# Weights of layer 1 and of both output projections split once ahead of use, kept in DRAM in two parts, and loaded in both parts

## The chip, the core and the metric

One NeuronCore of a Trainium2 chip runs the whole program in one launch. The metric is the device time in microseconds (us) of one execution, median of three. The engines are TensorE (PE, matrix products; PEld is its weight load), VectorE (DVE), ScalarE (ACT), GpSimd (POOL) and SyncE (SP), which here issues nearly all DMA transfers. Each engine works through its own instruction list in order and waits on semaphores.

## What is computed

Two layers of a streaming encoder in fp32, for 2048 prompt frames and 64 frames of a running stream (width D = 1024, 8 heads). Cut to what matters here:

```python
def hgrn_layer(x, S0, ...):                      # layer 0
    q, fx, i, z = jnp.split(rms_norm(x) @ w_in, 4)   # w0: 1024 x 4096
    f = lb + (1 - lb) * sigmoid(fx); k = 1 - f
    o, S = gla(q, k, i, log(f), S0)              # gated linear attention, blocks of 16
    return x + (rms_norm(o) * silu(z)) @ w_out   # wo0: 1024 x 1024

def diff_attn_layer(x, k_past, v_past, ...):     # layer 1
    q, k, v, z = jnp.split(rms_norm(x) @ w_in, 4)    # w1: 1024 x 4096
    p = softmax(rms_norm(q) @ rms_norm(k).T * 64 ** -0.5 - slope * dist)  # two maps per head
    o = (p[:, 0] - lam * p[:, 1]) @ v
    return x + (rms_norm(o) * (1 - lam_init) * silu(z)) @ w_out  # wo1: 1024 x 1024
```

Prompt frames attend causally by chunks of 64; the 64 sample frames attend to 2048 cached keys. Outputs are both layers' result, the new keys and values and the new states.

## The kernel before, in words

**Precision.** Each fp32 product is made of fp32r products: an operand is held as a high part (rounded to fp32r) and a low part (the rest), and `mm3` (L110 to L112) adds hi·hi, hi·lo and lo·hi. So every weight tile has to be split once: `split_w` copies the raw tile to the high half of a tile `w` of 128x2048 (ACT, L132) and subtracts that from the raw tile into the low half (L135, on POOL, on DVE, or half on each). For the output projections ACT first multiplies the raw tile by a scale per row (L131).

**Layer 0** (before about 1050 us) runs four chunks of 512 frames; in each, eight steps, one for each head: projection, gated scores, values, norm. In chunk 0 the w0 weights are loaded raw (`want`, `load_raw`), split, used, and stored in both parts in the DRAM tensor `w0_d`. Chunks 1 to 3 load both parts from there as 1 MB (`w<-w_d`) into a ring of NRING = 6 tiles. A step lasts some 24 us; the first and fifth step of a chunk, which also project values for four heads, last some 46 us. Then comes the output projection of layer 0 (`out_units`), whose eight weight tiles are loaded raw (0.5 MB) and split near the last steps of chunk 3.

**Layer 1** runs head after head, 17 tiles of frames each (16 of 128 prompt frames and one of the 64 sample frames), some 181 us a head: `project`, `turn`, `scores`, `values` and `norms` of different tiles, mixed by a plan that is written out for PE. Each tile's input `ht` is loaded from `h1_d`. The four weight tiles of the next head are loaded raw and split while the last tiles of a head are projected (`raw1` at tile NT-4, `split1` at tiles NT-2 and NT-1, subtractions half on DVE, half on POOL). The six first tiles of the second output projection are split the same way at the end of the last head (`split1` with h = H, on POOL), and the last two when attention ends (`open_rest`). Attention of the sample frames over the cache and the output projection follow.

**Order.** PE's order is written by hand (`manual_schedule`). The order on DVE, ACT, POOL and SP is chosen by the scheduler from the dependences, within the bounds that the pools set: a tile with `bufs=3` takes one of three buffers in turn, and its writer waits until the buffer's last reader is done. `dma` (L54) puts every transfer on SP's one list.

## Time and profile before

| | before |
|---|---|
| median of 3 executions | 3035.18 us (3032.98 to 3035.47) |
| the profiled execution | 3037.97 us, of which the span from first to last instruction is 3035.9 us |
| mean granted TensorE clock | 0.983 |
| busy share of the span | PE 96%, PEld 80%, DVE 65%, ACT 44%, POOL 25% |
| DMA | 494.10 MB, mean 163 GB/s |

The profile was taken on one execution, 2.8 us above the median; sums are made against 3037.97 us and then moved by that difference. Busy shares are means over stages that differ much: layer 0 to about 1056 us, its output projection to about 1263 us, layer 1's heads to about 2720 us, then the sample frames and the output projection.

### The profile page before, as it was taken

The page shows a single profiled execution, that of the slowest core. Times are in us where ns is not written, and L with a number is a line of the kernel's source. Part 1 is how long each engine was busy: PE and PEld are TensorE (multiplying, and loading weights), DVE is VectorE, ACT ScalarE, POOL GpSimd, SP SyncE. Part 2 cuts the span into 40 slices and gives each one's busy share as a digit, 9 for nine tenths or more (in the row PEclk, how much of TensorE's full clock was granted, in tenths as well). Part 3 has the DMA queues.
Part 4 walks back from the last instruction along what each step waited for, and adds up shares of the span by engine and source line. Part 5 has one row for each costly group of instructions (what it writes and reads, how often), then busy time and mean ns, then how long its engine had stood idle before and what let it go on. Part 6 is the DMA issues. An engine that isn't in the chain of part 4 may idle for free.

```text
span 3035.9 us, 49261 instructions
## 1 busy us (share of the span) xinstructions
PE 2917.5 (96%) x17258; PEld 2423.9 (80%) x17258; DVE 1974.7 (65%) x5598; ACT 1339.1 (44%) x3089; POOL 754.1 (25%) x841
## 2 busy tenths in 40 slices
PE   7999999999999899999999999999999999979898
PEld 5778888887899788787888878788887888867666
DVE  4765546546454744478687786868778686772673
ACT  3332122212211322356565565656656565553562
POOL 4330000000000200233333333332332333333451
PEclk8999999999999999999999999999999999989899
DMA  9554444444334266754444445444453544525653
GB/s 351 191 215 165 168 157 143 181 156 146 129 115 151 102 224 218 245 177 138 159 140 156 158 136 164 142 155 136 144 178 121 162 135 155 160 84 162 201 168 120
DMA packets 196679, 494.10 MB, mean 163 GB/s; under 512 B 27088, under 2 KB 114000, under 8 KB 161360
## 3 DMA queue, kind: packets, MB, share of 16 engines
q1 hardware_dynamic: 196432, 490.95, 48.3%
q8 instruction: 137, 2.24, 0.3%
q14 instruction: 110, 0.90, 0.1%
HBM read 352.45 MB, written 104.86 MB: 151 GB/s over the span
## 4 chain that ended last, share of the span: by engine, by line
PE 85%; DVE 7%; issue 2%; DMA 2%; POOL 2%; ACT 1%; SPq 0%; DVEq 0%; ACTq 0%; POOLq 0%
PE psproj L110 19%; PE psproj L112 18%; PE psproj L111 18%; PE psX L807 4%; PE psX L808 4%; PE psX L852 3%; PE psS L404 2%; PE psO L111 2%; PE psO L110 2%; PE psO L112 2%; PE psX L103 1%; DVE e L811 1%; PE psX L519 1%; PE psX L768 1%; DMA gs<-g_d 1%
## 5 line engine op out<-in xcount | busy, mean ns | idle before, releaser
L110 PE MATMUL psproj<-w,ht 128*128 128x512 f32 x1024 | 429.9, 420 | 0.3 <-DVE e L831 0.3
L112 PE MATMUL psproj<-w,ht 128*128 128x512 f32 x1024 | 403.7, 394 | 0.0
L111 PE MATMUL psproj<-w,ht 128*128 128x512 f32 x1024 | 403.7, 394 | 0.0
L816 ACT ACTIVATE e<-e,st 128x1024 f32<-128x1024 f32 (+7 forms) x384 | 343.2, 898 | 107.4 <-DVE st L811 107.3
L110 PE MATMUL psproj<-hT,w 128*128 128x512 f32 (+1 forms) x960 | 361.4, 376 | 0.0
L111 PE MATMUL psproj<-hT,w 128*128 128x512 f32 (+1 forms) x960 | 340.0, 354 | 0.0
L112 PE MATMUL psproj<-hT,w 128*128 128x512 f32 (+1 forms) x960 | 339.7, 354 | 0.0
L89 POOL TENSOR_TENSOR rs<-var,mhalf 128x4 f32<-128x4 f32 (+3 forms) x208 | 203.1, 978 | 432.0 <-DVE var L88 227.8
L811 DVE CUSTOM_DVE_ANT_0 e<-psX,dist,st 128x512 f32<-128x512 f32 (+3 forms) x384 | 248.1, 646 | 65.7 <-PE psX L808 59.8
L807 PE MATMUL psX<-kg,qt 128*128 128x512 f32 (+3 forms) x640 | 244.2, 382 | 6.8 <-DVE at L855 6.1
L854 ACT ACTIVATE at<-psX 128x512 fp32r<-128x512 f32 (+2 forms) x320 | 169.6, 531 | 168.2 <-PE psX L852 166.6
L808 PE MATMUL psX<-kg,qt 128*128 128x512 f32 (+3 forms) x640 | 237.5, 371 | 0.0
L811 DVE CUSTOM_DVE_ANT_0 e<-psX,dist 128x512 f32<-128x512 f32 (+3 forms) x256 | 163.0, 637 | 106.1 <-PE psX L808 104.0
L855 DVE TENSOR_TENSOR at<-psX,at 128x512 fp32r<-128x512 f32 (+2 forms) x320 | 193.7, 606 | 53.5 <-ACT at L854 51.6
L112 PEld LDWEIGHTS psproj<-w,ht 128*128 128x128 f32 x1024 | 192.5, 188 | 44.9
L110 PE MATMUL psproj<-w,gs 128*128 128x512 f32 x512 | 214.4, 419 | 7.0 <-ACT gs L573 7.0
L112 PE MATMUL psproj<-w,gs 128*128 128x512 f32 x512 | 206.2, 403 | 7.3 <-DVE gs L575 6.2
L111 PEld LDWEIGHTS psproj<-w,ht 128*128 128x128 f32 x1024 | 194.2, 190 | 15.8
L110 PEld LDWEIGHTS psproj<-w,ht 128*128 128x128 f32 x1024 | 193.7, 189 | 16.2 <-DVE st L829 0.7
L135 POOL TENSOR_TENSOR w<-wraw,w 128x1024 fp32r<-128x1024 f32 (+1 forms) x80 | 163.2, 2047 | 167.9 <-ACT w L132 158.1
L110 PEld LDWEIGHTS psproj<-hT,w 128*128 128x128 f32 x960 | 181.5, 189 | 29.1
L111 PE MATMUL psproj<-w,gs 128*128 128x512 f32 x512 | 204.4, 399 | 0.0
(245 smaller groups left out, 6618.6 us busy)
## 6 DMA issues: line engine op xcount, KB each, us to landing
ht<-h_d SPq DMA_DIRECT2D x128, 1024.0 KB, 5.1
w<-w_d SPq DMA_DIRECT2D x96, 1024.0 KB, 4.9
w_d<-w SPq DMA_DIRECT2D x32, 1024.0 KB, 4.9
qt<-qx SPq DMA_DIRECT2D x512, 64.0 KB, 2.1
gs<-g_d SPq DMA_DIRECT2D x44, 512.0 KB, 4.1
wraw<-in_w SPq DMA_DIRECT2D x32, 512.0 KB, 4.5
h_d<-hs SPq DMA_DIRECT2D x16, 1024.0 KB, 4.1
out_kvp<-raw SPq DMA_DIRECT2D x128, 128.0 KB, 1.8
```

The source lines that it names most:

```text
L89: G.tensor_tensor(out, v[:np_, :n], mhalf[:np_, :n], ALU.pow)
L110: T.matmul(out, l[0], r[0], start=first, stop=False)
L111: T.matmul(out, l[0], r[1], start=False, stop=False)
L112: T.matmul(out, l[1], r[0], start=False, stop=last)
L135: e.tensor_tensor(w[:, x * m:(x + 1) * m, 1], raw[:, x * m:(x + 1) * m], w[:, x * m:(x + 1) * m, 0], ALU.subtract)
L807: T.matmul(s[:, :w], qt[:, m, 0], kgt[:, m, :w], start=True, stop=False)
L808: T.matmul(s[:, :w], qt[:, m, 1], kgt[:, m, :w], start=False, stop=True)
L811: V.tensor_tensor_reduce(out=e[:, o:o + w], in0=s[:, :w], in1=dist[:, x0:x0 + w], scale=slope, scalar=3e38 if b["prev"] is None else b["pr ...
L816: A.activation(b["e"][m, hf][:, :n], b["e"][m, hf][:, :n], AF.Exp, bias=mn, scale=-1.0, accum_out=st4[:, 8 + 2 * hf + m:9 + 2 * hf + m])
L852: T.transpose(t[:, k * P:(k + 1) * P], b["a"][r][kt // 8][:, (kt % 8) * P:(kt % 8 + 1) * P], ident)
L854: A.activation(at[:, 0, :n, r], tv, AF.Copy)
L855: V.tensor_tensor(at[:, 1, :n, r], tv, at[:, 0, :n, r], ALU.subtract)
```

## The change

The weights of layer 1 and of both output projections (48 raw tiles of 0.5 MB) get the treatment of layer 0's own: 48 units `presplit`, two to a step, are written into the steps of chunks 1 to 3. Each loads a raw tile, makes the high part on ACT (two 128x512 copies) and the low part on DVE in place (two 128x512 subtractions), and stores both to new DRAM tensors `wo_d` and `w1_d` (two stores of 0.5 MB). Where these weights are used, `load_w` loads both parts as 1 MB. Raw and high parts share one tag of three buffers, which moves from the pool `wp` to `l0`. In layer 1 the next head's weights are loaded from tile NT-8 on, and the last of the four of each head after head 0 gets a buffer of its own (`wx`). `split_w` stays for w0 in chunk 0.

```diff
@@ -67,6 +67,8 @@
     h1_d = dram.tile([NT, P, 2, NK, P], F32, name="h1_d")
     sm_d = dram.tile([H, TS, 512], F32, name="sm_d")
     w0_d = dram.tile([H, 7, P, 2048], F32, name="w0_d")
+    w1_d = dram.tile([H, 4, P, 2048], F32, name="w1_d")
+    wo_d = dram.tile([2, 8, P, 2048], F32, name="wo_d")
 
     ident = const.tile([P, P], F32, name="ident")
     ones = const.tile([P, 1], F32, name="ones")
@@ -117,18 +119,22 @@
         T.matmul(out, l, r[1], start=False, stop=last)
 
     def load_raw(src, n):
-        raw = wp.tile([P, 1024], F32, tag="raw", bufs=NRAW, name="wraw")
+        raw = l0.tile([P, 1024], F32, tag="raw", bufs=NRAW, name="wraw")
         raw = raw.rearrange("p (k n) -> p k n", n=n)
         dma(raw, src)
         return raw
 
-    def split_w(raw, n, pool=None, scale=None, engines=(G,)):
-
-        w = (pool or wp).tile([P, 2048], F32R, tag="w", bufs=2 if pool else NRING, name="w")
+    def load_w(src, n, pool=None, tag="w", bufs=None):
+
+        w = (pool or wp).tile([P, 2048], F32R, tag=tag, bufs=bufs or NRING, name="w")
+        dma(w.bitcast(F32), src)
+        return w.rearrange("p (k a n) -> p k a n", a=2, n=n)
+
+    def split_w(raw, n, engines=(G,)):
+
+        w = wp.tile([P, 2048], F32R, tag="w", bufs=NRING, name="w")
         w = w.rearrange("p (k a n) -> p k a n", a=2, n=n)
         nk = 1024 // n
-        for k in range(nk if scale is not None else 0):
-            A.activation(raw[:, k], raw[:, k], AF.Copy, scale=scale[:, k:k + 1])
         A.activation(w[:, :, 0], raw, AF.Copy)
         m = nk // len(engines)
         for x, e in enumerate(engines):
@@ -192,13 +198,10 @@
             c, h, s = key = wlist[wnext[0]]
             wnext[0] += 1
             if c != "out" and c > 0:
-                w = wp.tile([P, 2048], F32R, tag="w", bufs=NRING, name="w")
-                dma(w.bitcast(F32), w0_d[h, s])
-                n = P if s < 3 else 512
-                ws[key] = w.rearrange("p (k a n) -> p k a n", a=2, n=n)
+                ws[key] = load_w(w0_d[h, s], P if s < 3 else 512)
                 continue
             if c == "out":
-                ws[key] = split_w(load_raw(out_src(0, h, s), 512), 512, scale=osc[:, 0, 2 * s:2 * s + 2])
+                ws[key] = load_w(wo_d[0, 4 * h + s], 512)
             elif s < 3:
                 ws[key] = split_w(load_raw(I["w0h"][h, s].rearrange("p (k n) -> p k n", k=NK), P), P, engines=engines)
             else:
@@ -206,6 +209,36 @@
                 ws[key] = split_w(load_raw(I["w0v"][h // 4, k:k + 2].rearrange("k p n -> p k n"), 512), 512, engines=engines)
             if c == 0:
                 dma(w0_d[h, s], ws[key].rearrange("p k a n -> p (k a n)").bitcast(F32))
+
+
+    plist = [(0, n) for n in range(8)] + [(2 + h, k) for h in range(H) for k in range(4)] + [(1, n) for n in range(8)]
+
+    def presplit(x):
+
+        ly, n = plist[x]
+        b = {}
+
+        def load():
+            src = out_src(ly, n // 4, n % 4) if ly < 2 else I["w1"][ly - 2, 2 * n:2 * n + 2].rearrange("k p n -> p k n")
+            b["raw"] = load_raw(src, 512)
+
+        def split():
+            raw = b["raw"]
+            hi = l0.tile([P, 1024], F32, tag="raw", bufs=NRAW, name="whi").rearrange("p (k n) -> p k n", n=512)
+            dst = (wo_d[ly, n] if ly < 2 else w1_d[ly - 2, n]).rearrange("p (k a n) -> p k a n", a=2, n=512)
+            for k in range(2):
+                h, r = hi[:, k].bitcast(F32R), raw[:, k]
+                if ly < 2:
+                    sc = osc[:, ly, 2 * (n % 4) + k:2 * (n % 4) + k + 1]
+                    A.activation(h, r, AF.Copy, scale=sc)
+                    V.scalar_tensor_tensor(out=r.bitcast(F32R), in0=r, scalar=sc, in1=h, op0=ALU.mult, op1=ALU.subtract)
+                else:
+                    A.activation(h, r, AF.Copy)
+                    V.tensor_tensor(r.bitcast(F32R), r, h, ALU.subtract)
+            dma(dst[:, :, 0], hi)
+            dma(dst[:, :, 1], raw)
+
+        return [(1, load), (1, split)]
 
     def norm0(c, n):
         ti = cxs[c]["tiles"][n]
@@ -633,21 +666,17 @@
             units += [(0.43, lambda g=g: turn(ti, g)) for g in range(2)]
         return units
 
-    def raw1(h, k):
-
-        if h < H:
-            ctxs[h]["raw"][k] = load_raw(I["w1"][h, 2 * k:2 * k + 2].rearrange("k p n -> p k n"), 512)
-        elif k < NRING:
-            cx1["raw"][k] = load_raw(out_src(1, k // 4, k % 4), 512)
-
-    def split1(h, k):
-        if h < H:
-            ctxs[h]["w"][k] = split_w(ctxs[h]["raw"].pop(k), 512, engines=(V, G))
-        elif k < NRING:
-            cx1["w"][k // 4, k % 4] = split_w(cx1["raw"].pop(k), 512, scale=osc[:, 1, 2 * (k % 4):2 * (k % 4) + 2])
-
-    cx1 = dict(ly=1, w={}, raw={})
-    ctxs = {h: dict(w=[None] * 4, kg={}, v={}, q={}, z={}, ht={}, raw={}) for h in range(H)}
+    def load1(h, k):
+
+        if h == H:
+            cx1["w"][k // 4, k % 4] = load_w(wo_d[1, k], 512)
+        elif h > 0 and k == 3:
+            ctxs[h]["w"][k] = load_w(w1_d[h, k], 512, r1, "wx", 1)
+        else:
+            ctxs[h]["w"][k] = load_w(w1_d[h, k], 512)
+
+    cx1 = dict(ly=1, w={})
+    ctxs = {h: dict(w=[None] * 4, kg={}, v={}, q={}, z={}, ht={}) for h in range(H)}
 
     s1, s1b, r0s, r1s, so = (ExitStack() for _ in range(5))
     r1 = l1 = l1e = l1b = psum1 = None
@@ -702,15 +731,16 @@
             else:
                 mm2(cx["pp"], cx["ht"][i][:, 0, k], rhs, k == 0, k == NK - 1)
             if k % 2:
-                if i == NT - 4 and k < 4:
-                    raw1(h + 1, k // 2)
-                if i == NT - 2 and k < 4:
-                    split1(h + 1, k // 2)
-                    raw1(h + 1, k // 2 + 2)
-                if i == NT - 1 and (k < 4 or h == H - 1):
-                    split1(h + 1, k // 2 + 2)
-                    if h == H - 1:
-                        raw1(H, k // 2 + 4)
+
+                early = [0, 1] + [2] * (h > 0) + [3] * (h == 0)
+                if NT - 8 <= i < NT - 8 + len(early) and k == 3:
+                    load1(h + 1, early[i - NT + 8])
+                if i == NT - 1 and h == H - 1 and k < 6:
+                    load1(H, 3 + k // 2)
+                elif i == NT - 1 and h == 0 and k == 1:
+                    load1(1, 2)
+                elif i == NT - 1 and 0 < h < H - 1 and k == NK - 1:
+                    load1(h + 1, 3)
             if k == NK - 1:
                 cx["ht"].pop(i)
                 finish(cx["pp"])
@@ -1068,7 +1098,7 @@
         s1.close()
         op2, cx1["split"] = pool(s3, "op2"), V
         for k in range(NRING, 8):
-            cx1["w"][1, k % 4] = split_w(load_raw(out_src(1, 1, k % 4), 512), 512, pool=op2, scale=osc[:, 1, 2 * (k % 4):2 * (k % 4) + 2])
+            cx1["w"][1, k % 4] = load_w(wo_d[1, k], 512, op2, bufs=2)
         open_decode()
 
     def open_rows():
@@ -1115,7 +1145,8 @@
                 for _, step in main[:2] + side[:1]:
                     step()
                 main, side = main[2:], side[1:]
-            weave((0, 1, main), (0, 1, side))
+            x = 2 * (n - H)
+            weave((0, 1, main), (0, 1, side), (0, 1, presplit(x) + presplit(x + 1) if c else []))
             if h == 1 and c > 0:
                 rms0(c - 1)
         sh.close()
@@ -1124,7 +1155,7 @@
         work0 = [(ti, (0, 1)) for ti in [0, 1, 2, NT - 1] + list(range(3, NT - 1))]
         out_load(cx0, *work0[0])
         for n in range(NRING, 8):
-            cx0["w"][1, n % 4] = split_w(load_raw(out_src(0, 1, n % 4), 512), 512, pool=op, scale=osc[:, 0, 2 * (n % 4):2 * (n % 4) + 2])
+            cx0["w"][1, n % 4] = load_w(wo_d[0, n], 512, op, bufs=2)
         cx0["wbc"] = op.tile([P, D], F32, tag="wbc", bufs=1, name="wbc1")
         dma(cx0["wbc"], I["norm_bc"][1])
         weave((0, 0.9, side0(*steps[-1])), (OPS, 1, out_units(cx0, work0, 0, ps0) + out_units(cx0, work0, 1, ps0)))
@@ -1143,15 +1174,11 @@
         op_last = ub[16:]
         out_load(cx0, *work0[-1])
         load_ht(0)
-        for k in range(2):
-            raw1(0, k)
         for _, step in ua[:6] + prev[:1] + ua[6:8] + ub[:1] + prev[1:] + ub[1:8]:
             step()
+        for k in range(4):
+            load1(0, k)
         dma(dist, I["dist"])
-        for k in range(4):
-            split1(0, k)
-            if k < 2:
-                raw1(0, k + 2)
         for _, step in ua[8:16] + ub[8:13] + last[:1] + ub[13:15] + last[1:] + ub[15:16]:
             step()
         for _, _, step in sorted(plan, key=lambda x: x[:2]):
```

In the built programs PE has the same instructions in the same order. On DVE the 96 subtractions stand from the fifth head of chunk 0 to the fourth head of chunk 2, since the scheduler moves them ahead of their place in the text; the order shows no presplit in chunk 3. Names carry buffer numbers, which differ between the two; line numbers too (L396 of the change is L363 of before, L446 is L413, L841 is L811, L861 is L831, L885 is L855, L801 is L771).

DVE in chunk 1, where the products of keys k with decays F of one step are made, before:

```order
L363 TENSOR_TENSOR k_3026<-k_3026,F_3250 128x128x2
L413 COPY_PREDICATED attc_3251<-masks_92,psS_3296 128x64x2
L363 TENSOR_TENSOR k_3026<-k_3026,F_3250 128x64x4
L413 COPY_PREDICATED attc_3251<-masks_92,psS_3296 128x32x4 x2
L363 TENSOR_TENSOR k_3026<-k_3026,F_3250 128x32x8
L413 COPY_PREDICATED attc_3251<-masks_92,psS_3354 128x16x8
L363 TENSOR_TENSOR k_3026<-k_3026,F_3250 128x16x16
L413 COPY_PREDICATED attc_3251<-masks_92,psS_3354 128x8x16 x2
L363 TENSOR_TENSOR Q_3252<-Q_3252,F_3250 128x8x32
L363 TENSOR_TENSOR k_3026<-k_3026,F_3250 128x8x32
L363 TENSOR_TENSOR Q_3252<-Q_3252,F_3250 128x4x64
L363 TENSOR_TENSOR k_3026<-k_3026,F_3250 128x4x64
```

and the same place with the change (L237 is the presplit's subtraction):

```order
L237 TENSOR_TENSOR wraw_5173<-wraw_5173,whi_5220 128x512 x2
L237 TENSOR_TENSOR wraw_5295<-wraw_5295,whi_5359 128x512 x2
L396 TENSOR_TENSOR k_3082<-k_3082,F_3324 128x32x8
L446 COPY_PREDICATED attc_3325<-masks_94,psS_3430 128x16x8
L396 TENSOR_TENSOR k_3082<-k_3082,F_3324 128x16x16
L446 COPY_PREDICATED attc_3325<-masks_94,psS_3430 128x8x16 x2
L237 TENSOR_TENSOR wraw_5403<-wraw_5403,whi_5450 128x512 x2
L396 TENSOR_TENSOR Q_3326<-Q_3326,F_3324 128x8x32
L396 TENSOR_TENSOR k_3082<-k_3082,F_3324 128x8x32
L396 TENSOR_TENSOR Q_3326<-Q_3326,F_3324 128x4x64
L396 TENSOR_TENSOR k_3082<-k_3082,F_3324 128x4x64
L237 TENSOR_TENSOR wraw_5535<-wraw_5535,whi_5624 128x512 x2
```

Four presplits, eight subtractions, now stand between or just around the products k<-k,F of one step; PE's score products wait for these.

SP at the start of layer 1, before (ht is a tile's input, h_d what turn stores, x_d the residual, wraw raw weights, out_kvp an output of keys and values):

```order
L54 DMA wraw_10863<-in_w1 128x2x512
L54 DMA wraw_12213<-in_w1 128x2x512
L54 DMA wraw_12235<-in_w1 128x2x512
L54 DMA wraw_12509<-in_w1 128x2x512
L54 DMA x1_d_65<-xt_10701 128x1024
L54 DMA wraw_12543<-in_w1 128x2x512
L54 DMA wraw_14425<-in_w1 128x2x512
L54 DMA x1_d_65<-xt_10776 128x1024
L54 DMA h1_d_66<-hs_10923 128x2048
L54 DMA ht_11028<-h1_d_66 128x2048
L54 DMA ht_11072<-h1_d_66 128x2048
L54 DMA h1_d_66<-hs_10981 128x2048
L54 DMA out_kvp<-raw_11000 128x256
```

and with the change:

```order
L54 DMA w_11244<-w1_d_69 128x2048
L54 DMA w_11246<-w1_d_69 128x2048
L54 DMA w_11248<-w1_d_69 128x2048
L54 DMA x1_d_65<-xt_11095 128x1024
L54 DMA w_12096<-w1_d_69 128x2048
L54 DMA w_12227<-w1_d_69 128x2048
L54 DMA x1_d_65<-xt_11170 128x1024
L54 DMA h1_d_66<-hs_11301 128x2048
L54 DMA h1_d_66<-hs_11359 128x2048
L54 DMA out_kvp<-raw_11378 128x256
L54 DMA ht_11406<-h1_d_66 128x2048
L54 DMA ht_11450<-h1_d_66 128x2048
```

The 0.5 MB raw loads are 1 MB loads of both parts, and the two ht loads that stood ahead of the last h1_d store now come behind it and behind the first out_kvp store, which waits for POOL.

DVE at one of the seven changes of head, near 1590 us in the trace of before (e, st and at belong to the softmax of the last tiles of one head), before:

```order
L135 TENSOR_TENSOR w_14896<-wraw_14721,w_14896 128x512
L831 SCALAR_TENSOR_TENSOR e_14706<-e_14774,st4_14705,e_14706 128x1024
L831 SCALAR_TENSOR_TENSOR e_14736<-e_14831,st4_14705,e_14736 128x640
L811 ISA e_14917,st4_14881<-psX_14935,dist_9715,st4_14881 128x256
L811 ISA st4_14881 128x1
L135 TENSOR_TENSOR w_14924<-wraw_14755,w_14924 128x512
L855 TENSOR_TENSOR at_14928<-psX_14929,at_14928 128x3x128
L771 SCALAR_TENSOR_TENSOR qx_14947<-psX_14944,wq_98,qx_14947 128x128
L811 ISA e_14962,st4_14881<-psX_14963,dist_9715 128x512
L811 ISA st4_14881 128x1
L135 TENSOR_TENSOR w_16929<-wraw_16637,w_16929 128x512
L811 ISA e_14962,st4_14881<-psX_14972,dist_9715,st4_14881 128x512
```

and with the change:

```order
L861 SCALAR_TENSOR_TENSOR e_15070<-e_15126,st4_15069,e_15070 128x1024
L861 SCALAR_TENSOR_TENSOR e_15094<-e_15183,st4_15069,e_15094 128x640
L841 ISA e_15265,st4_15233<-psX_15279,dist_10109,st4_15233 128x256
L841 ISA st4_15233 128x1
L885 TENSOR_TENSOR at_15272<-psX_15273,at_15272 128x3x128
L801 SCALAR_TENSOR_TENSOR qx_15291<-psX_15288,wq_100,qx_15291 128x128
L841 ISA e_15306,st4_15233<-psX_15307,dist_10109 128x512
L841 ISA st4_15233 128x1
L841 ISA e_15306,st4_15233<-psX_15316,dist_10109,st4_15233 128x512
L841 ISA st4_15233 128x1
L841 ISA e_15329,st4_15233<-psX_15330,dist_10109,st4_15233 128x512
L841 ISA st4_15233 128x1
```

The subtractions of L135 are gone, and the softmax rows stand in the same order.

## Rows read from the trace of the kernel before

**Rows 1.** PE's waits, whole span: for what, us in total, times, longest.

```profile
PE psX L852 <- DVE st L811: 13.7, 8, 3.0
...
PE psX L852 <- DVE e L831: 11.0, 8, 4.4
...
PE psX L807 <- DVE at L855: 6.1, 7, 1.8
```

**Rows 2.** Layer 0: us, busy PE PEld DVE ACT POOL, clock, DMA share, GB/s.

```profile
0.00:50.00 50.00, 34.62 (x135) 26.87 (x136) 18.22 (x43) 21.45 (x32) 18.89 (x16) 0.86 0.92 342
...
450.00:700.00 250.00, 250.00 (x1675) 201.01 (x1674) 135.18 (x400) 56.38 (x119) 13.20 (x13) 1.00 0.44 159
```

**Rows 3.** Groups by line: busy us, mean ns of one, idle before and releaser.

```profile
L135 POOL TENSOR_TENSOR w<-wraw,w 128x1024 fp32r<-128x1024 f32 (+1 forms) x80 | 163.2, 2047 | 167.9 <-ACT w L132 158.1 <-PE psX L489 6.7 <-PE psproj L112 2.7
...
L131 ACT ACTIVATE wraw<-wraw,osc 128x512 f32<-128x512 f32 x32 | 21.5, 714 | 8.8 <-DMA wraw<-in_wo 8.7
```

**Rows 4.** End of layer 0, DVE, POOL in order of time: start us, us, operation.

```profile
1017.09 0.52 DVE L363 TENSOR_TENSOR k<-k,F 128x256 f32<-128x256 f32 x2
...
1042.16 3.77 DVE L363 TENSOR_TENSOR k<-k,f 128x256 f32<-128x256 f32 x2
...
1046.63 4.09 DVE L363 TENSOR_TENSOR k<-k,F 128x256 f32<-128x256 f32 x2
...
1043.34 7.34 POOL L135 TENSOR_TENSOR w<-wraw,w 128x1024 fp32r<-128x1024 f32 x3
```

**Rows 5.** PE's waits from 1020 to 1060 us.

```profile
PE psS L404 <- DVE k L363: 7.9, 3, 5.0
```

**Rows 6.** Stretches at the lower clock, columns as in rows 2.

```profile
1051.50:1056.10 4.60, 4.56 (x25) 3.79 (x26) 3.53 (x15) 0.00 (x0) 0.00 (x0) 0.50 0.59 219
...
1595.40:1598.80 3.40, 3.24 (x11) 2.88 (x12) 3.33 (x10) 1.90 (x7) 0.00 (x0) 0.50 0.65 213
...
2697.90:2704.70 6.80, 6.59 (x27) 6.20 (x28) 5.03 (x15) 4.55 (x10) 2.71 (x4) 0.50 0.07 17
```

**Rows 7.** DVE late in one head of layer 1 and at the change to the next.

```profile
1563.68 2.08 DVE L831 SCALAR_TENSOR_TENSOR e<-e,st 128x1024 f32<-128x1024 f32 x2
...
1590.16 3.11 DVE L831 SCALAR_TENSOR_TENSOR e<-e,st 128x1024 f32<-128x1024 f32 x2
...
1596.20 0.68 DVE L135 TENSOR_TENSOR w<-wraw,w 128x512 fp32r<-128x512 f32 x1
```

**Rows 8.** PE's waits from 2680 to 2725 us, at the end of the last head.

```profile
PE psX L852 <- DVE e L831: 4.4, 1, 4.4
...
PE psX L852 <- DVE st L811: 3.0, 1, 3.0
```

**Rows 9.** Start of layer 1, SP and PE in order of time.

```profile
1268.60 4.89 SPq L54 DMA_DIRECT2D ht<-h_d  x2
...
1274.48 0.34 SPq L54 DMA_DIRECT2D out_kvp<-raw  x1
...
1275.18 0.40 PE L110 MATMUL psproj<-w,ht 128*128 128x512 f32 x1
```

**Rows 10.** DMA issues: KB each, median us from issue to landing.

```profile
ht<-h_d SPq DMA_DIRECT2D x128, 1024.0 KB, 5.1
...
wraw<-in_w SPq DMA_DIRECT2D x32, 512.0 KB, 4.5
...
wraw<-in_w0h SPq DMA_DIRECT2D x24, 512.0 KB, 6.6
```

**Rows 11.** DVE between which, by the order, the first and last presplits come.

```profile
220.53 0.28 DVE L384 COPY M<-Q 128x256 f32<-128x256 f32 x1
...
626.41 0.43 DVE L434 TENSOR_TENSOR q<-q,f 128x256 f32<-128x256 f32 x1 [1.46 <-ACT q L291]
```

**Rows 12.** The last key product of a step in chunk 1, and its user on PE.

```profile
382.24 0.42 DVE L363 TENSOR_TENSOR k<-k,F 128x256 f32<-128x256 f32 x1
...
382.89 0.68 PE L480 MATMUL psX<-Q,k 128*64 128x64 f32 x8
```

## The prediction

> **What bounds the kernel now.** I read the page first: PE is busy nearly all of the span, so a change gains only where PE waits or runs slowly, and loses wherever it makes PE wait. Then the table of stretches: in layer 0 between 450 and 700 us PE is busy 250.00 of 250.00 us, DVE (the third busy time in such a row) 135.18, ACT 56.38, and the DMA engines are at a share of 0.44 for 159 GB/s [rows 2]. Nothing is to be gained there. Then PE's waits over the whole span: the greatest in layer 1 are for softmax work of DVE, 13.7, 11.0 and 6.1 us in 7 or 8 pieces each [rows 1], one for each change of head and one for the end of the last head. There the kernel splits weights. The timeline of these places shows how: a pair of L831 that takes 2.08 us in the middle of a head takes 3.11 us at a change [rows 7], and at the end of layer 0 pairs of L363 that take 0.52 us take 3.77 and 4.09 us while POOL runs three subtractions L135 for 7.34 us [rows 4]. DVE and POOL hold each other up. Behind such waits the granted clock falls: three stretches of 4.60, 3.40 and 6.80 us were run at 0.50, the level of 1.2 GHz, with PE busy for 4.56, 3.24 and 6.59 us [rows 6]; a stretch like the second stands at each change of head.
>
> **What the change removes.** All splits of w1, wo0 and wo1 leave these places, among them 48 of POOL's 80 subtractions L135 of 2.05 us on average [rows 3] and the four on DVE at each change of head.
>
> *End of layer 0.* PE waits 7.9 us for k L363 [rows 5]. The first slow pair begins 1.2 us before POOL's L135, so of its excess 3.77 − 0.52 = 3.25 us about 2.0 are due to L135; the second pair's excess is 4.09 − 0.52 = 3.57 [rows 4]. Together 5.6 us, less than the wait. The half-clock stretch behind it costs half of 4.56 us, 2.3 [rows 6]. Term: −8 (bounds −4, if the clock falls anyway and a third of the wait stays, and −11, wait and clock whole).
>
> By the Trainium skill, page "SBUF — State Buffer", section "Who interferes with whom", a DVE operation with two SBUF inputs and a GpSimd operation that reads SBUF exclude each other for a whole instruction. The pairs above agree: 0.52 us alone, 4.09 beside L135. By that rule the new subtractions, which have two SBUF inputs as well, would be blocked where they meet POOL's remaining splits in chunk 0, where POOL is busy 18.89 of the first 50 us [rows 2]; a dozen of the 96 stand in chunk 0, and with 2.05 us [rows 3] for two in five of them that would be some 10 us of DVE time, inside the bounds for layer 0 below.
>
> *Seven changes of head.* Without the end of the last head (3.0 and 4.4 us [rows 8]) the three waits of rows 1 come to 10.7 + 6.6 + 6.1 = 23.4 us, 3.3 a change. The four L135 on DVE, 0.68 us each when undisturbed, and the 1.03 us that the pair L831 loses [rows 7] make 3.7 us of DVE time just ahead of these waits, more than the waits. I take four fifths of 23.4, since the softmax chain itself stays: 19. Half of 3.24 us of clock [rows 6] is 1.6, times seven 11. Term: −30 (−12 to −40). The new loads are 1 MB at 5.1 us [rows 10] where raw ones were 0.5 MB; three of four are issued some tiles ahead, under the products of the tiles between; the fourth goes with the head's last product and is used three quarters of a tile later, some 8 us (181 us a head over 17 tiles). I cost them at nothing; without that cover a change loses up to 5 us.
>
> *End of the last head.* Waits of 7.4 us [rows 8] and half of 6.59 us [rows 6]: −10 (−5 to −20, if the waits for gs just behind it shrink too).
>
> **What it adds.** *Start of layer 1.* The two ht loads that were issued from 1268.60 on now stand behind the first out_kvp, which went at 1274.48; so the first goes at about 1274.9 and lands 5.1 us later, at 1280.0, while PE starts on that tile at 1275.18 [rows 9, 10]. Queued behind it on PE is everything. Term: +5 (0, if out_kvp goes earlier since POOL is freer, to +9).
>
> *Start of the sample frames.* Two 1 MB loads of wo1 stand on SP's list just ahead of inputs that PE waits for; one such load lands in 5.1 us [rows 10]. +3 (0 to +6).
>
> *Layer 0.* By the order the presplits don't spread over the last three chunks: they lie between rows that start at 220.53 and 626.41 us [rows 11], 48 in some 406 us, one in 8.5 us. Three costs meet there.
>
> First, cover. Each brings two subtractions like L135, 0.68 us [rows 7], and two copies like L131, 0.71 us [rows 3]: 65 us on DVE, 69 on ACT. There is room on average, but not in the chain: the last key product ends at 382.66 and PE takes it at 382.89 [rows 12], 0.2 us of cover, and the order puts up to four presplits between such products. If one piece in six comes late by its length less the cover, 96 / 6 × 0.5 = 8 us; with the longer steps of values, better covered, I take 10.
>
> Second, the loop. Raw and high parts share three buffers, so a presplit's high part waits for the store of the raw part before it: per presplit 0.71 + 2 × 0.68 = 2.1 us of ACT and DVE and one store. The trace has no such store; the nearest rows are 0.5 MB transfers of 4.5 us and, at chunk 0's load, 6.6 us [rows 10]. So 6.6 to 8.7 us, against 8.5 that there are: slack of 1.9 at one end, short by 0.2 × 48 = 10 us at the other. As all engines go in order, a late store stops ACT and DVE, and they PE.
>
> Third, DMA. 48 × 1.57 MB in 406 us is 186 GB/s, on top of 159 makes 345, as much as the first 50 us moved at a share of 0.92 (342 GB/s) [rows 2]. So I take the loaded end, nearest in load, and with the uneven places (four in one step) 15 us for the loop. Term for layer 0: +25 (0, all covered, to +75, stores of 8 us: 10 us of cover and 48 × 1.6 rounded down).
>
> By the Trainium skill, page "DMA: Bandwidth & Descriptors", section "Where 436 GB/s comes from", HBM transfers of a core are bound at about 358 GB/s; the first 50 us (342 at 0.92) agree in order of size. By that rule the 345 fit with 4% to spare and transfers would queue, which speaks against this change: it is the mechanism of rival C, whose price and chance are worked out from the rows alone.
>
> **Sum.** −8 − 30 − 10 + 5 + 3 + 25 = −15: from 3037.97 to 3023 in a profiled execution. That execution stands 2.8 us above the median, so 3020 for the median, 0.5% faster. A measurement of this kernel can tell about 0.2%, 6 us, from no change.
>
> **Rivals.** *A, the forecast*: 3005 to 3030, chance 0.44.
>
> *B, layer 0 hides it all.* For it: DVE is busy 54%, ACT 23% and the DMA engines 44% there [rows 2], and PE has other products to do. Against: the cover of 0.2 us [rows 12]. Without the +25 the sum is −40: 2995, and down to 2980 with the ends of the gains. Chance 0.16.
>
> *C, the other side: the presplit loop paces layer 0.* If a store takes more than 6.4 us (8.5 − 2.1) under load, each of the 48 presplits is late and holds ACT, DVE and SP. The other terms come to −40; with 10 us of cover the gain is gone when 48 × (store − 6.4) = 30, at a store of 7.0 us. At 7.5 us the loop costs 53 and the sum is +23: 3058. For it: 6.6 us at chunk 0's load [rows 10] and 345 GB/s; against: layer 0's loads are issued well ahead, and PE can go on while SP is late. Chance 0.23.
>
> *D, the changes of head keep their waits.* If the softmax chain and the tile of sample frames, not L135, set them, only 12 of the 30 come, and the sum is +3: about no change, 3038. For it: the clock falls after quite short waits; against: 3.7 us of DVE time goes from just there. Chance 0.17.
>
> A and B make it faster, D in part; C slower. Faster by over 0.2%: 0.61; within: 0.16; slower: 0.23. The range 2988 to 3050 leaves out the far ends of B and C; A's own range is 3005 to 3030.
>
> **What would show it.** In the changed kernel's profile: no split of weights after chunk 0's other than the presplits; L831 pairs at about 2.1 us at the changes of head, PE's three waits of rows 1 below half, fewer half-clock stretches; a new wait of some 5 us for ht near the start of layer 1; in layer 0 from 220 to 650 us a DMA share near 0.9, PE waits for k L363's counterpart, ACT waiting for buffers of the stores, and chunk 2's end late by some 25 us. I am wrong if layer 0 is not late at all or by over 50 us, or if waits at the changes of head stay though the splits are gone.

## The result, and the profile after

The change takes 2997.72 us (median of four, 2996.45 to 3003.42) against 3034.83 us: a ratio of 0.9882, with an interval of 0.9865 to 0.9899. The profiled execution took 2998.95 us, its span 2997.1 us, against 3037.97 and 3035.9. It is 1.2% faster, where 0.5% was forecast: the direction holds, the gain is over twice the forecast one.

PE runs the same 17258 matmuls in the same order in both kernels, so the time between the same two matmuls can be compared. The table cuts the span by the times of before; "PE idle" is the change in the time that PE stood between matmuls.

| stretch of before, us | forecast | measured | of it PE idle |
|---|---|---|---|
| 0 to 220, chunk 0 | 0 | −0.6 | −0.1 |
| 220 to 1000, layer 0 | +25 | +16.1 | +12.0 |
| 1000 to 1060, its end | −8 | −6.5 | −4.7 |
| 1060 to 1262, output projection | 0 | −0.3 | −0.3 |
| 1262 to 1300, start of layer 1 | +5 | +5.3 | +3.2 |
| seven changes of head | −30 | −42.3 | −24.9 |
| 2665 to 2735, end of the last head | −10 | −12.8 | −10.4 |
| 2735 to 2830, start of the sample frames | +3 | +4.2 | +2.6 |
| 2830 to the end | 0 | −2.1 | −1.2 |

The sum is −39.0; forecast was −15. Two terms make most of the difference: the changes of head gained 12 us more, layer 0 lost 9 us less.

The table compares one execution of each kernel. The runs below repeat parts of it, and say how far each row can be trusted. The changes of head took 42.2 to 42.3 us less in all five later kernels that leave them as the change has them. Layer 0 (220 to 1000 us) took 15.2 to 20.0 us more in the six that leave it so, and repeated itself within 0.01 us in the two that are the kernel before there. Behind 2665 us single executions differ more: those same two kernels, in which nothing behind 2665 us was edited, took 16.1 and 5.8 us less for the last three rows than the profile of before, so the gain at the end of the last head is anything from 7 to 13 us.

PE's waits in the change, whole span (for what, us in total, times, longest), which answer to [rows 1]:

```profile
PE psX L513 <- DVE k L396: 7.3, 6, 2.6
...
PE psproj L112 <- DMA ht<-h_d: 4.3, 1, 4.3
...
PE psO L113 <- DVE at L885: 3.3, 8, 0.7
...
PE psX L882 <- DVE e L861: 3.1, 1, 3.1
```

The 13.7 and 6.1 us of [rows 1] are gone, the 11.0 us are down to one wait of 3.1 at the end of the last head. New are 7.3 us for key products in layer 0, one wait of 4.3 us for ht, and smaller ones. The table of stretches (length, busy PE PEld DVE ACT POOL, granted clock, DMA share, GB/s) shows layer 0 twice, the start of layer 1, one change of head and the end of the last head:

```profile
250.00:300.00 50.00, 48.00 (x324) 38.05 (x321) 33.19 (x82) 19.68 (x39) 2.07 (x2) 0.97 0.91 311
550.00:600.00 50.00, 49.59 (x305) 40.23 (x303) 31.73 (x84) 14.03 (x29) 1.50 (x1) 1.00 0.96 361
1271.20:1280.00 8.80, 8.80 (x46) 7.26 (x45) 4.48 (x8) 3.63 (x8) 0.54 (x1) 1.00 1.02 422
1579.20:1624.10 44.90, 44.08 (x259) 37.72 (x258) 39.34 (x118) 29.39 (x69) 15.50 (x19) 1.00 0.61 210
2637.10:2694.30 57.20, 49.58 (x265) 41.25 (x264) 41.97 (x111) 31.37 (x66) 17.25 (x16) 0.94 0.39 125
```

In layer 0 the DMA engines are at 0.91 and 0.96, where before they were at 0.44 [rows 2]. At the change of head PE is busy for 44.08 of 44.90 us at full clock, where a stretch at 0.50 stood [rows 6]. The pair of L831 that took 3.11 us there [rows 7] is the pair L861 now, on DVE in order of time:

```profile
1598.16 2.08 DVE L861 SCALAR_TENSOR_TENSOR e<-e,st 128x1024 f32<-128x1024 f32 x2
```

It takes what it takes in the middle of a head. Where layer 0 loses time, DVE, ACT and PE in order of time show one of the places:

```profile
387.52 0.69 DVE L237 TENSOR_TENSOR wraw<-wraw,whi 128x512 fp32r<-128x512 f32 x1 [1.68 <-ACT whi L236]
...
388.33 0.69 DVE L237 TENSOR_TENSOR wraw<-wraw,whi 128x512 fp32r<-128x512 f32 x1
```

```profile
386.86 1.16 ACT L236 ACTIVATE whi<-wraw 128x512 fp32r<-128x512 f32 x2 [2.36 <-DMA w_d<-whi]
```

```profile
391.14 0.68 PE L513 MATMUL psX<-Q,k 128*64 128x64 f32 x8 [2.60 <-DVE k L396]
```

ACT has the raw tile but waits 2.36 us for a buffer, until the store of an earlier high part is done (`w_d<-whi`); DVE waits 1.68 us for ACT, works 2 × 0.69 us on the presplit, and PE's score products wait 2.60 us for the key product behind that. The summary of ACT's line L236 (what it waited for, and who waited for it, us and times) and the transfers (KB, us to landing) say how common this is:

```profile
L236 ACT ACTIVATE whi<-wraw x64: 612/621/635, 292.3 to 568.5; 128x512 fp32r<-128x512 f32 x64
...
  DMA wraw<-in_w: 45.4, 19
  DMA w_d<-whi: 26.6, 7
...
  DVE wraw L237: 52.6, 26
```

The larger wait is for raw loads. They are late in part because SP holds them back: a load, too, needs a buffer, and SP waits for the store of the low part that is still in it. SP's own wait for these stores, 219.7 to 686.4 us:

```profile
SPq L54 <- DMA w_d<-wraw: 28.6, 10, 5.7
```

```profile
w<-w_d SPq DMA_DIRECT2D x128, 1024.0 KB, 6.3
...
wraw<-in_w SPq DMA_DIRECT2D x32, 512.0 KB, 6.3
w_d<-whi SPq DMA_DIRECT2D x32, 512.0 KB, 5.7
w_d<-wraw SPq DMA_DIRECT2D x32, 512.0 KB, 6.8
```

Transfers of layer 0 take 5.7 to 6.8 us; in_w, loaded in layer 1 before, took 4.5 [rows 10]. At the start of layer 1, SP and PE in order of time:

```profile
1274.11 6.22 SPq L54 DMA_DIRECT2D h_d<-hs  x2
1283.21 0.34 SPq L54 DMA_DIRECT2D out_kvp<-raw  x1
1283.64 0.88 SPq L54 DMA_DIRECT2D ht<-h_d  x2
```

```profile
1289.06 0.77 PE L112 MATMUL psproj<-w,ht 128*128 128x512 f32 x1 [4.29 <-DMA ht<-h_d]
```

The first ht goes at 1283.64, behind out_kvp at 1283.21, and PE starts on it 5.4 us later, after a wait of 4.29 us. This is the wait that was forecast, with its size; whether its cause is the one that was forecast is tested below.

### The profile page after: what moved, and what is told of

It reads as the page before. It is cut to its first block, busy times and chain, and to the rows that moved or that the text cites. A ratio compares the mean times of both kernels' runs of the same rounds, so it can differ in the third digit from the quotient of the medians.

```text
span 2997.1 us, 49564 instructions
## 1 busy us (share of the span) xinstructions
PE 2902.5 (97%) x17258; PEld 2414.6 (81%) x17258; DVE 1966.5 (66%) x5662; ACT 1325.9 (44%) x3105; POOL 683.5 (23%) x793
## 5 line engine op out<-in xcount | busy, mean ns | idle before, releaser
L91 POOL TENSOR_TENSOR rs<-var,mhalf 128x4 f32<-128x4 f32 (+3 forms) x208 | 219.1, 1055 | 414.0 <-DVE var L90 200.6
L841 DVE CUSTOM_DVE_ANT_0 e<-psX,dist,st 128x512 f32<-128x512 f32 (+3 forms) x384 | 248.0, 646 | 61.2 <-PE psX L838 54.4
L837 PE MATMUL psX<-kg,qt 128*128 128x512 f32 (+3 forms) x640 | 239.8, 375 | 0.0
L838 PE MATMUL psX<-kg,qt 128*128 128x512 f32 (+3 forms) x640 | 234.5, 366 | 0.0
L885 DVE TENSOR_TENSOR at<-psX,at 128x512 fp32r<-128x512 f32 (+2 forms) x320 | 194.1, 607 | 52.4 <-ACT at L884 50.5
L841 DVE CUSTOM_DVE_ANT_0 e<-psX,dist 128x512 f32<-128x512 f32 (+3 forms) x256 | 163.1, 637 | 95.9 <-PE psX L838 93.6
L112 PEld LDWEIGHTS psproj<-hT,w 128*128 128x128 f32 x960 | 181.7, 189 | 29.3
L114 PEld LDWEIGHTS psproj<-hT,w 128*128 128x128 f32 x960 | 181.7, 189 | 24.3
```

Of the source, the lines that this page charges most:

```text
L91: G.tensor_tensor(out, v[:np_, :n], mhalf[:np_, :n], ALU.pow)
L112: T.matmul(out, l[0], r[0], start=first, stop=False)
L114: T.matmul(out, l[1], r[0], start=False, stop=last)
L837: T.matmul(s[:, :w], qt[:, m, 0], kgt[:, m, :w], start=True, stop=False)
L838: T.matmul(s[:, :w], qt[:, m, 1], kgt[:, m, :w], start=False, stop=True)
L841: V.tensor_tensor_reduce(out=e[:, o:o + w], in0=s[:, :w], in1=dist[:, x0:x0 + w], scale=slope, scalar=3e38 if b["prev"] is None else b["pr ...
```

## Experiments

Theories on layer 0's loss: the **loop** (three buffers, so that ACT and then DVE stop for transfers), **occupancy** (the subtractions' own time in the chain) and **DMA** (the engines are full). On the changes of head: DVE's **time**, the **lock** between DVE and POOL, and **ACT**'s copies. Each kernel ran once with a profile, the last one in five rounds. Stretches are compared by matched matmuls, as above.

**Four buffers.**

```diff
-    NRING, NRAW = 6, 3
+    NRING, NRAW = 6, 4
...
-    xn = cx["xn", ti] = cx["pool"].tile([P, D], F32, tag="xn", name="xn")
+    xn = cx["xn", ti] = cx["pool"].tile([P, D], F32, tag="xn", bufs=1, name="xn")
```

> The change with four buffers instead of three for raw and high parts (and one buffer instead of two for xn in layer 0's output projection, to make room). Stage looked at: the part of layer 0 that lay from 220 to 670 us before, which takes 16.7 us longer in the change. Theory loop (a high part waits for a store or a load of the presplits, ACT and then DVE stop behind it): ACT's waits for stores go, the stage is late by 5 to 10 us instead of 16.7. Rival occupancy (the subtractions' own 0.7 us each sit in the chain of key products): still 14 to 18. Rival DMA (the DMA engines are full, at a share of 0.86 to 0.96): still 14 to 20, since more is asked of them at once.

220 to 670 us of before takes 2.9 us more than before, not 16.7; PE's idle time there falls from 13.2 to 3.2 us. The same stretch as a window, in this run and then in the change, and what ACT's line L236 waited for here and who waited for it:

```profile
215.50:668.40 452.90, 449.69 (x2998) 360.98 (x2999) 292.77 (x792) 154.01 (x305) 26.55 (x23) 1.00 0.89 323
```

```profile
219.70:686.40 466.70, 453.51 (x2999) 361.57 (x3000) 297.56 (x793) 152.82 (x305) 26.44 (x23) 1.00 0.89 315
```

```profile
  DMA wraw<-in_w: 31.1, 17
...
  DVE wraw L237: 24.3, 12
```

ACT waits for no store any more; SP still does, but its longest wait for one is 3.4 us, not 5.7. The DMA engines are as full as in the change (0.89 in both), and DVE does the same work. So it is the loop that cost most: DMA and occupancy together are left with 2.9 us here, and with 5.7 us in the last kernel below, which has the same four buffers. Chunk 0 gains too (0 to 220: 4.9 us less than before), as its own raw tiles share the buffers. The output projection of layer 0, with one buffer less for xn, takes 3.4 us more than before. The whole took 2980.71 us.

**Presplits over three chunks** (the copy with a scale likewise).

```diff
-                    A.activation(h, r, AF.Copy)
+                    with tc.issue_after(mark[0].ins):
+                        A.activation(h, r, AF.Copy)
```

> The change, with each high part ordered behind the newest sigmoid of f in the text on ACT, so that the 48 presplits lie in chunks 1 to 3 instead of from late in chunk 0 to early in chunk 2. Theory loop: twelve and more us for each presplit instead of 8.5, so waits for the transfers go: layer 0 as a whole (0 to 1000 us of before) late by 3 to 8 us instead of 15.6. Rival occupancy: the same 96 subtractions in the same kind of chain, late by 12 to 18 us, now spread to 1000 us. Rival DMA: share falls to about 0.75, late by under 5 us.

0 to 1000 us is 13.2 us late (7.9 from 220 to 670, 4.7 from 670 to 1000, 0.7 before), against 15.6 in the change. That is outside the 3 to 8 us of the loop theory and inside the 12 to 18 us of its rival occupancy. Two of PE's waits there:

```profile
PE psX L537 <- ACT kTs L526: 5.8, 7, 1.7
PE psX L515 <- DVE k L398: 0.9, 1, 0.9
```

PE's waits for key products before its score products are mostly gone (L515 here, 7.3 us at L513 in the change), but ACT still waits for stores (20.3 us in 11 pieces for the high parts of w1), and PE now waits more for kTs, a copy on ACT (5.8 us against 2.5). The edge pins the high parts to one place in ACT's order, behind the sigmoid, where they stand ahead of work that PE wants. So this run decides nothing between loop and occupancy; it says that more room in time is worth little if the pieces stand in a bad place.

**Subtractions of w1 on POOL.**

```diff
-                    V.tensor_tensor(r.bitcast(F32R), r, h, ALU.subtract)
+                    G.tensor_tensor(r.bitcast(F32R), r, h, ALU.subtract)
```

> The change with the 64 subtractions of w1's presplits on POOL instead of DVE; those of both wo stay on DVE. Theory occupancy: two thirds of DVE's new work are gone from the chain, 220 to 670 us late by 5 to 8 us instead of 16.7. Rival loop: the loop gets longer by POOL's slower subtraction, ACT still waits for transfers, but DVE no longer stops for them: 8 to 14 us if ACT passes the delay on, under 6 if only DVE does. Rival lock (DVE and POOL exclude each other): DVE's operations of two inputs wait for POOL for 1.3 us each time, late by 15 us or more.

220 to 670 us is 14.5 us late, against 16.7. What L236 waited for and who waited for it:

```profile
  DMA wraw<-in_w: 29.4, 16
  DMA w_d<-whi: 11.0, 2
...
  POOL wraw L237: 144.3, 26
```

POOL, not DVE, now waits for ACT, and two thirds of the new work on DVE are gone (64 subtractions of 0.69 us, 44 us), yet only 2.2 us come back. So occupancy of DVE is not the main cause; ACT, which still waits for transfers, is left to pass the delay on. The rival lock, 15 us or more, is missed by 0.5 us and not excluded: beside POOL's subtractions DVE's products of Q by F (128x256) take 493 ns on average from 219.5 to 686 us, 433 in the change, and those of k by f 794, not 562, some 9 us in all.

**The kernel before, splits of w1 on POOL alone.**

```diff
-            ctxs[h]["w"][k] = split_w(ctxs[h]["raw"].pop(k), 512, engines=(V, G))
+            ctxs[h]["w"][k] = split_w(ctxs[h]["raw"].pop(k), 512, engines=(G,))
```

> The kernel before, with the splits of w1 at the changes of head on POOL alone instead of half on DVE, half on POOL. In seven changes PE waits 30.7 us in all before and 5.7 in the change, which gains 42.3 us there with the clock. Theory DVE time (the four subtractions on DVE make its softmax rows late): waits fall to under 12 us and most of the gain is there, 25 to 40 us faster in these seven places. Rival lock (POOL holds the shared port and blocks DVE): POOL runs twice as long, waits stay at 25 to 45 us, from 10 us faster to 15 slower. Rival ACT (the four copies of 1.05 us make its exponentials late): waits stay at 20 to 31 us.

From 1300 to 2665 us, the seven changes, it takes 4.5 us more than before, and PE's idle time rises from 30.7 to 38.3 us. So DVE's own subtractions are not the cause by themselves. That DVE was not freed by this is shown further down.

**Parts put back, one engine at a time.** Four pieces for a change, placed in the text where `split1` stood; for ACT, then with one line in its place for POOL, for DVE, and with both:

```diff
+            if k % 2 and NT - 2 <= i < NT and k < 4 and h < H - 1:
+                wn = ctxs[h + 1]["w"][k // 2]
+                junk = r1.tile([P, 1024], F32R, tag="junk", bufs=1, name="junk").rearrange("p (k n) -> p k n", n=512)
+                A.activation(junk, wn[:, :, 0], AF.Copy)
...
+                G.tensor_tensor(junk[:, 0], wn[:, 0, 0], wn[:, 0, 1], ALU.subtract)
...
+                V.tensor_tensor(junk[:, 0], wn[:, 0, 0], wn[:, 0, 1], ALU.subtract)
```

> The change, with ACT's part of the old work put back at the changes of head: four copies of 128x1024 a change (as L132 did), from loaded weights into a tile that nobody reads; outputs stay whole. Seven changes took 42.3 us less in the change than before, and PE's waits there fell from 30.7 to 5.7 us. Theory ACT (the copies make the exponentials late): waits back to 20 us or more, 20 to 35 us of the 42 lost. Rivals DVE time and lock: waits under 10 us, under 6 us lost.

> The change, with POOL's part put back: four subtractions of 128x512 a change on loaded weights, into a tile that nobody reads. Theory lock (a POOL subtraction holds up DVE's softmax rows of two inputs): waits back to 12 us or more, 10 to 25 us lost. Rivals ACT and DVE time: waits under 9 us, under 4 us lost.

> The change, with DVE's part put back: four subtractions of 128x512 a change on loaded weights, into a tile that nobody reads. Theory DVE time (four times 0.68 us ahead of the softmax rows): waits back to 12 us or more, 10 to 25 us lost. Rivals ACT and lock: waits under 9 us, under 4 us lost. The run in which POOL alone split the weights kept the waits, which speaks against DVE time.

> The change, with DVE's and POOL's parts both put back, without ACT's. If the two add up, the time lost is the sum of what each alone loses. If they hold each other up (lock), it is more than the sum by 5 us or over: up to 30 us. If ACT's copies are what counts, under 6 us lost.

The scheduler issues each set one change earlier than its place, so the seventh change got none: six are compared, 1390 to 2340 us of before, where the change needs 915.7 us and before 949.9, 34.2 more.

| kernel | us over the change | PE idle there |
|---|---|---|
| the change | 0 | 4.9 |
| ACT's part put back | 14.2 | 14.0 |
| POOL's | 8.8 | 12.4 |
| DVE's | 12.9 | 14.9 |
| POOL's and DVE's | 23.9 | 23.9 |
| all three (below) | 46.8 | 29.8 |
| before, DVE alone (below) | 33.5 | 26.0 |
| before, POOL alone | 38.1 | 31.2 |
| before | 34.2 | 24.1 |

Put back alone, each engine's part costs 8.8 to 14.2 us, and POOL with DVE cost 23.9, against 21.7 for the sum of both. None of the three theories, which each gave one engine the most and the others nearly nothing, fits all three runs: DVE's part cost what DVE's time had said (10 to 25 us), but ACT's, for which it had said under 6, cost more, and POOL's over twice its 4.

But the parts do not stand where the splits stood. At the change near 1590 us, on the scale of before, the four subtractions on DVE begin between 1589.2 and 1601.4 us, and those put back between 1596.1 and 1603.6. The longest of the old waits, of PE for st, comes back in none of these runs. In the six changes it is, in before, with POOL alone and with DVE alone:

```profile
PE psX L852 <- DVE st L811: 9.1, 6, 1.5
```

```profile
PE psX L852 <- DVE st L811: 18.1, 6, 3.0
```

```profile
PE psX L852 <- DVE st L811: 4.1, 6, 0.7
```

So these runs show what such work costs a few microseconds later, and that no engine's part is free there. What each engine's share was of what the change gained is not shown.

**The kernel before, splits on DVE alone; and all three parts put back.**

```diff
-            ctxs[h]["w"][k] = split_w(ctxs[h]["raw"].pop(k), 512, engines=(V, G))
+            ctxs[h]["w"][k] = split_w(ctxs[h]["raw"].pop(k), 512, engines=(V,))
```

> The kernel before, with the splits of w1 on DVE alone: eight subtractions of 128x512 a change of head, POOL none. In the middle of layer 1 (six changes, 1390 to 2340 us of before) before takes 34.1 us more than the change. If POOL's hold on DVE were the main cause, this kernel is faster there than before, by 5 us or more, and the rows L831 of 128x1024 fall from 1445 ns to the change's 1313. If engine time adds up (four more subtractions for DVE at the 2.1 us a change that four cost in the run with DVE's part put back, four less for POOL at 1.5): about 4 us slower there than before, with L831 at 1313 all the same.

> The change with ACT's, DVE's and POOL's parts all put back at the changes of head, as useless work behind each other (subtractions behind the copies). Alone they lost 14.2, 12.6 and 8.8 us in the six changes. If the three engines' time is all that the change removed there: about 30 to 38 us lost, as much as the 34.1 between before and the change. If the raw loads or the clock count for more: under 25.

DVE alone takes 0.7 us less than before in the six changes: neither 5 us less, as the lock had it, nor 4 more, as added engine time had it. DVE's rows in the six changes (busy us, mean ns) say why; before, with DVE alone, with POOL alone, and in the change:

```profile
L831 DVE SCALAR_TENSOR_TENSOR e<-e,st 128x1024 f32<-128x1024 f32 (+4 forms) x126 | 129.2, 1052 | 1.1
L135 DVE TENSOR_TENSOR w<-wraw,w 128x512 fp32r<-128x512 f32 x24 | 25.0, 1040 | 0.0
```

```profile
L831 DVE SCALAR_TENSOR_TENSOR e<-e,st 128x1024 f32<-128x1024 f32 (+4 forms) x126 | 122.9, 1004 | 0.9
L135 DVE TENSOR_TENSOR w<-wraw,w 128x1024 fp32r<-128x1024 f32 x24 | 29.3, 1222 | 0.0
```

```profile
L831 DVE SCALAR_TENSOR_TENSOR e<-e,st 128x1024 f32<-128x1024 f32 (+4 forms) x126 | 145.9, 1185 | 0.9
```

```profile
L861 DVE SCALAR_TENSOR_TENSOR e<-e,st 128x1024 f32<-128x1024 f32 (+4 forms) x126 | 122.9, 1003 | 0.9
```

Against the change's 122.9 us, DVE is busy with these rows for 31.3 us more in before, 29.3 more with all subtractions on DVE, and 23.0 more with none. With half of them on POOL, those left on DVE take 1040 ns each, where they took 686 in the run with DVE's part put back. So being held up beside POOL, the lock, makes about half of the 31.3 us (6.3 in L831, 8.5 in the subtractions) and all of the 23.0, and giving half to POOL freed DVE of next to nothing. By the Trainium skill, "SBUF — State Buffer", "Who interferes with whom", the two block each other for a whole instruction; these means agree in that DVE's rows get longer beside POOL, and cannot show whether it is for a whole one.

All three put back cost 46.8 us, more than the 35.9 of the parts, than before's 34.2 and than the 38 that was expected at most. PE's idle time adds up (24.9 us over the change; the parts alone 9.1, 7.5 and 10.0, together 26.6). PE waits there again for DVE, though not for st:

```profile
PE psX L888 <- DVE e L867: 14.9, 6, 3.0
PE psO L113 <- DVE at L891: 12.2, 10, 3.0
```

The rest is clock: in the six changes PE's clock stood at 0.50 for 47.7 us in this run, 23.9 in before, 3.4 with ACT's part alone and not at all with POOL's or DVE's alone. So waits add, and with all of them together the clock falls as well. A rival stays for what this run costs above before: the tile that nobody reads has one buffer, and ACT waited 10.0 us in the whole run for DVE and POOL to be done with it.

**ht ahead of out_kvp; and both remedies.** For the first, `load_ht` keeps its transfer in `mark[0]`:

```diff
+            if (h, i) == (0, 0):
+                with tc.issue_after(mark[0].ins):
+                    dma(O["kvp"][h, i * P:(i + 1) * P], raw[:, 128:384])
...
```

> The change, with one edge more on SP: the first out_kvp is ordered behind the ht loads. The start of layer 1 (1262 to 1300 us of before) takes 5.3 us longer in the change. Theory order (ht stands behind out_kvp, which waits for POOL until 1283.2): ht goes at about 1280.4 instead of 1283.6, PE's wait of 4.3 us falls to about 1, the stage is 1 to 2.5 us longer than before. Rival DMA (the transfers there are late because the DMA engines are full, at a share of 0.88 to 1.02): the wait stays at 3 us or more.

SP and PE of this run in order of time (layer 0 ran some 4 us later in it, before this place):

```profile
1280.60 6.22 SPq L54 DMA_DIRECT2D h_d<-hs  x2
1286.91 1.26 SPq L54 DMA_DIRECT2D ht<-h_d  x2
1289.70 0.34 SPq L54 DMA_DIRECT2D out_kvp<-raw  x1
```

```profile
1294.99 0.77 PE L112 MATMUL psproj<-w,ht 128*128 128x512 f32 x1 [3.74 <-DMA ht<-h_d]
```

ht goes as soon as the second h_d is off, 3.2 us earlier than in the change, counted from the stretch's first matmul, but PE starts on it after 8.1 us instead of 5.4. The wait is 3.74 us, and the stretch 4.7 us longer than before. The nine runs with the change's own order wait 3.8 to 5.4 us there and take 4.0 to 6.9 us longer, so ht ahead of out_kvp gains next to nothing: that order made the issue late, as forecast, but it is not what PE's wait comes from. The rival DMA had the size right. The second h_d and two ht, 1 MB each, are now issued close together.

The runs differ in something else. Before, and with DVE alone, both ht go ahead of the second h_d, and PE does not wait for ht. With POOL alone, whose edit also moves the splits at this place, they go behind it, though ahead of out_kvp. SP and PE's wait in that run:

```profile
1268.04 5.35 SPq L54 DMA_DIRECT2D h_d<-hs  x2
1273.44 2.62 SPq L54 DMA_DIRECT2D ht<-h_d  x2
1276.27 5.88 SPq L54 DMA_DIRECT2D out_kvp<-raw  x2
```

```profile
PE psproj L110 <- DMA ht<-h_d: 4.1, 1, 4.1
```

So the kernel before has the wait too when ht stands behind the second h_d, and the stretch is 6.5 us longer than in its other run. In all twelve runs with that order PE waits for ht, 3.7 to 5.4 us; in the two without it, it does not. No run moved the second h_d alone, so this is a reading of the runs and not a test.

For the second, raw and high parts are taken from the pool `hp`, which is closed before the output projection:

```diff
-        raw = l0.tile([P, 1024], F32, tag="raw", bufs=NRAW, name="wraw")
+        raw = hp.tile([P, 1024], F32, tag="raw", bufs=NRAW, name="wraw")
...
```

> The change with four buffers for raw and high parts, now taken in the pool that is closed before the output projection (so that projection keeps its two xn buffers), and with the ht loads ahead of out_kvp. If the loop and the order are the causes, the gains add: layer 0 as with four buffers (about 15 us less than the change), the output projection as in the change, layer 1's start 3 to 4 us less: about 2979 us, 0.6 to 0.7% below the change and 1.8% below before. Rival DMA or occupancy: no more than 0.2% below the change.

2981.99 us (2973.18 to 2983.32) against 3031.51: a ratio of 0.9823, interval 0.9803 to 0.9844. It beats both kernels; the change stood at 0.9882, measured against before as well. 0 to 220 us takes 6.7 less than before, 220 to 670 5.7 more, the output projection of layer 0 0.3 less, the start of layer 1 3.9 more. So the buffers are what it gains by; the order of ht gives 1.4 us of the 3 to 4 that were expected, less than runs with one and the same order differ by.

## Why the prediction fell short

*End of layer 0* (−8) measured −6.5: right, by the steps given. *Start of the sample frames* (+3) measured +4.2, and 2.4 to 6.8 in the other runs with these loads: PE waits 3.7 us for sm, where it waited 1.6 before. *Start of layer 1* (+5) measured +5.3, but its step was wrong: it had the wait come from out_kvp ahead of ht, and with ht first PE still waits 3.74 us. The wait goes with ht behind the second h_d. That the size came out is luck. The last stretch, 2830 us to the end, costed at nothing, moved by −2.1; in runs that don't differ there it lay between 0.0 and −7.1, so it is no effect of the change.

*Seven changes of head* (−30, bounds −12 to −40) measured −42.3. This is the step that failed first, by the size of both its factors. "I take four fifths of 23.4, since the softmax chain itself stays": nothing stayed of these waits, and some of PE's wait for at at L111 went with them, so idle time fell by 24.9, not by 19. "Half of 3.24 us of clock", times seven, gave 11; eight such stretches of 3.4 us stood at the seven changes, none is left, and that is 13.7. The last 3.7 us lie in PE's busy time outside these stretches, not in its waits; what they are stays open. The working also laid all on DVE, with 3.7 us a change for four subtractions of 0.68 us and the pair L831. Beside POOL the subtractions took 1.04 us each, and with L831 it was 5.2 us a change (31.3 in six). ACT's four copies it left out; put back, a few microseconds later in the change, they cost as much as DVE's part. What their share was is not shown.

*Layer 0* (+25) measured +16.1. The mechanism was named rightly, and the four buffers show it: high parts, and raw loads with them, wait for stores in a loop of three buffers. Its size was not: of 10 us for cover and 15 for the loop, 2.9 and 5.7 us were left with four buffers for cover and all else, and by difference the loop cost 11 to 14 of the 16.7 us from 220 to 670. So cover is the term that was sized wrong. The step "if one piece in six comes late by its length less the cover" counted each piece as late by itself; that idle time of DVE between the pieces takes most of them is a reading that no run tests. The upper bound of +75 is a slip: its own terms, 10 and 48 × 1.6, make 87.

*End of the last head* (−10) measured −12.8, inside its bounds, and so is the whole range of 7 to 13 us that other executions of before leave.

The rivals: B gave 2995, close to the time, but its mechanism is wrong: layer 0 did lose 16 us, and that the changes of head gained 12 more than forecast brought the time there, which is luck. C had the mechanism, the loop paces layer 0, and its own price, 48 × (6.8 − 6.4) = 19 us for the slowest stores, is near what was lost. But the stores took 5.7 to 6.8 us, under the 7.0 at which C would have decided. By the Trainium skill, "DMA: Bandwidth & Descriptors", "Where 436 GB/s comes from", transfers with HBM are bound at about 358 GB/s a core; the rows here show 361 GB/s for 50 us and 422 for 8.8 us, so that rule was no bound in these stretches, and with one buffer more PE was 2.9 and 5.7 us late at means of 323 and 321. D is refuted.

## What to carry to other kernels

Work that is taken out of a crowded place is worth what it costs there on all engines together, and what the clock gives back once the waits are gone. Here the forecast looked at DVE, the engine that PE was waiting for, and came out too small, while to move the subtractions between DVE and POOL bought nothing. Work that is moved into a quiet place cost less by its engine time here than by its buffers: count the transfers in the loop from load to store, and give one buffer more than the mean rate asks for. A transfer moved forward in a full queue may land no sooner. A useless piece of work that is put back to price an engine is a test only if it stands where the old work stood.

## What the runs showed of the hardware

With four buffers the DMA engines ran at a mean share of 0.89 for some 450 us, and PE lost 2.9 us in one execution and 5.7 in another; with three, at the same share, it lost 16.7. The 0.5 MB loads of in_w took 6.3 us to land there, 4.5 in layer 1 before. Half of the subtractions given to POOL left DVE as long on the other half (25.0 us in six changes, and 6.3 more in L831) as on all of them by itself (29.3 us). The clock follows PE's waits, but not by their sum alone: 1.3 to 1.7 us of them put back at each change of head by one engine's work left it at full in all but one of eighteen places; the 3.2 us a change of before went with a stretch at 0.50 at each; the 3.2 us of POOL's and DVE's parts together with one at a single change of six. What tells the last two apart stays open.
